# Relative bias of a banded attention: turned by a product with a flip matrix, or read from copies in DRAM with a shorter row step

## The chip, the core and the metric

One core of a Trainium2 chip runs the kernel. The metric is the device time in microseconds, the median of several runs. The engines are TensorE (PE; its weight loads are listed as PEld), VectorE (DVE), ScalarE (ACT), GpSimd (POOL), and SyncE (SP), which issues every DMA of this kernel. Each engine runs its own instructions in a fixed order and waits on semaphores for the others. 16 DMA engines move the data.

## The reference, cut to what matters

The kernel computes one layer of a hybrid encoder for a prompt of 2048 tokens and a sample of 64: an RMS norm, one input projection (1024 to 4096), banded attention with 8 heads of 64 in one half, a gated linear recurrence with 4 heads of 128 in the other, an output projection with a residual, and a last RMS norm. The change concerns the bias that is added to the attention scores. It depends on the clipped distance of query and key alone:

```python
def band_attention(q, k, v, rel, valid, rel_bias):
    idx = jnp.clip(rel, -REL_CLIP, REL_CLIP) + REL_CLIP
    bias = rel_bias[:, idx].astype(jnp.float32)
    s = jnp.einsum('bnqhd,bnkhd->bnhqk', q, k).astype(jnp.float32) * ATTN_SCALE + bias
    s = jnp.where(valid[None, :, None], s, NEG_INF)
    p = jax.nn.softmax(s, axis=-1).astype(v.dtype)
    return jnp.einsum('bnhqk,bnkhd->bnqhd', p, v)
...
rel = jnp.arange(CHUNK)[:, None] + WINDOW_ROWS - band[None, :]
```

REL_CLIP is 128. So for a block of 128 queries the bias is a band matrix: the same for every block, with each row shifted by one against the row above, and one constant for all keys that are 128 or more back.

## The kernel before

**Tiles and stages.** The 2048 + 64 tokens are cut into four stages of 512 (the second has the sample's 64 beside them, SUPER). In each stage the 32 column tiles of the input projection are taken one after the other (JOBS): four groups g, and in each the four projections of a recurrence head (hf, hq, hi, hg) and the four of a pair of attention heads (pg, pq, pk, pv). One projection of a 512-token block is 24 products of 128x128 by 512: weights and inputs are each split into a high and a low part in float32r, and three of the four combinations are summed. The first stage loads the weights from the input (wraw), splits them on DVE (high part, a cast) and POOL (low part, four subtractions), and stores both parts in DRAM (wd); the later stages load wd. The weight tiles w are a ring of four, the raw tiles a ring of two. Between the projections of a group PE does the attention of pairs and the recurrences of heads that are ready. In the last stage the output projection follows, stored as seven products a pair of row blocks.

**The order.** The program is written by hand in generators, and a planner (class Plan, lines 52 to 237) runs them at trace time. It keeps a clock, charges each instruction an estimated duration on its engine, and lets a generator go on when the time that it asked for has come: `yield t` waits for the planned time t, `yield "D", t` waits until t and until DVE's planned queue is less than 600 ns ahead. What comes out is a fixed order on each engine. A DMA is planned (lines 204 to 208) as 520 ns after its issue, its bytes at 370 per ns behind the transfers planned earlier, and 2000 ns to land. `tk` holds tokens for shared buffers: "ck" a work tile of 128 x 512, "g" one PSUM bank that the recurrences use for all their small products.

**The bias.** The host lays rel_bias out as one row of 383 numbers for each head: 127 times the value of the farthest distance, then 256 values in order of falling distance. `load_bias` (lines 816 to 847) makes the tile `bias` of a pair of heads, [128, 2, 640], with the negative of the bias. It is spawned by `open_` of each pair (line 909). In the first stage, four times in all, it builds the tile and stores it in DRAM (biasd); in the later stages it only loads it. The build:

- line 825: SP loads `win`, in which partition i and head h hold numbers i to i + 255 of the head's row. Each partition starts one further than the one above. The bias needs the opposite: partition i must start at 127 - i.
- line 827: SP loads `far`, the first number of each row, to all partitions.
- lines 830 and 831: DVE fills columns 0 to 383 with the constant, one operation for each head.
- lines 833 to 835: PE multiplies `win` by `flip` (ones on the other diagonal), which turns the order of the partitions round, into the bank "g".
- line 839: DVE copies the bank to columns 384 to 639 with its sign changed.
- lines 841 and 842: DVE sets the columns that a chunk may not see to a large number.
- line 846: SP stores the tile.

`softmax_rows` (line 1013) does not start before `bias_at`, the planned time of the finished tile; DVE adds the bias to the scores there. `flip` is made once by POOL (lines 474 to 476).

Of the kernel before, what the change touches and what calls it, by code (L numbers as in the profile page):

```python
# [8 lines left out]
F32 = mybir.dt.float32  # L9
# [3 lines left out]
ALU = mybir.AluOpType  # L13
# [4 lines left out]
P = 128  # L18
D = 1024
# [353 lines left out]
def hymba_step(  # L373
# [24 lines left out]
    C = Plan()  # L398
    act, dve, pool, pe, sp = (Queue(C, e, x) for e, x in (("A", nc.scalar), ("D", nc.vector), ("P", nc.gpsimd),
                                                          ("T", nc.tensor), ("S", nc.sync)))  # L400
# [4 lines left out]
    cst = ctx.enter_context(tc.tile_pool(name="cst", bufs=1))  # L405
    wk = ctx.enter_context(tc.tile_pool(name="wk", bufs=2))
    dr = ctx.enter_context(tc.tile_pool(name="dr", bufs=1, space=DRAM))
# [5 lines left out]
    def T(pool_, shape, dt, tag, **kw):  # L413
        uid[0] += 1
        C.name(homes.get(id(pool_), ""), tag, kw.get("bufs") or 1, f"{tag}_{uid[0]}")
        return pool_.tile(list(shape), dt, tag=tag, name=f"{tag}_{uid[0]}", **kw)

    def psum(tag, shape=(P, 512), bufs=1):
        return T(ps, shape, F32, tag, bufs=bufs)
# [22 lines left out]
    def mm32(out, w, x):  # L442
        pe.matmul(out, w, x, start=True, stop=True)

    tk = {k: Tok(C, n) for k, n in dict(acc=2, s_ps=1, tr=2, pv=1, g=1, pr=PRB, ph=2, sig=2, vT=2, mixa=2,
                                     w=WBUFS, raw=RAWB, xn=XNB, kv=1, q=1, sga=2, bias=1, gf=1, gi=1, gg=1,
                                     ck=1, slot=4, x4=0, x5=0, rec=1).items()}
# [1 line left out]

    ident = T(cst, [P, P], F32, "ident")  # L450
    make_identity(nc, ident)
    flip = T(cst, [P, P], F32, "flip")
    ones = T(cst, [P, P], F32R, "ones")
    mask = T(cst, [P, P], U32, "mask")
    eps_t = T(cst, [P, 1], F32, "eps")
# [12 lines left out]
    def constants():  # L468
        pool.memset(eps_t, EPS)
        pool.memset(one_t, 1.0)  # L470
        maskf = asb[0][:, 0]
        pool.memset(maskf, 1.0)
        dve.tensor_copy(ones, maskf)
        pool.memset(flip, 1.0)
        pool.affine_select(out=flip, in_=flip, pattern=[[1, P]], compare_op=ALU.is_equal, fill=0.0,
                           base=-(P - 1), channel_multiplier=1)
        pool.affine_select(out=maskf, in_=maskf, pattern=[[1, P]], compare_op=ALU.is_ge, fill=0.0,
                           base=0, channel_multiplier=-1)
        dve.tensor_copy(mask, maskf)
        pool.memset(reset, 1.0)  # L480
        pool.memset(reset.rearrange("p (b t) -> p b t", t=32)[:, :, 0:1], 0.0)
        pool.memset(asb[0], 0.0)
# [333 lines left out]
    def load_bias(sb, p, d):  # L816
        yield from tk["bias"].get()
        nb = d.bias = T(wk, [P, 2, 640], F32, "bias", bufs=1)
        if sb:
            sp.dma_start(nb, biasd[p])  # L820
            d.bias_at = C.dma(655)
            return
        yield from tk["ck"].get()
        win = T(wk, [P, 4, P], F32, "ck", bufs=1).rearrange("p (h a) c -> p h (a c)", h=2)
        sp.dma_start(win, bass.AP(rel_rev.tensor, 2 * p * 383, [[1, P], [383, 2], [1, 256]]))
        far = T(wk, [P, 2], F32, "far", bufs=1)
        sp.dma_start(far, bass.AP(rel_rev.tensor, 2 * p * 383, [[0, P], [383, 2]]))
        t = C.dma(400)
        yield "D", t
        for h in range(2):  # L830
            dve.tensor_scalar(nb[:, h, 0:384], reset[:, :384], 0.0, far[:, h : h + 1], ALU.mult, ALU.subtract)
        C.dve(600)
        yield from tk["g"].get()
        pw = psum("g")
        pe.matmul(pw, flip, win.rearrange("p h c -> p (h c)"), start=True, stop=True)
        tk["ck"].put()
        t = C.pe()
        yield "D", t
        dve.tensor_scalar(nb[:, :, 384:640], pw.rearrange("p (h c) -> p h c", h=2), -1.0, None, ALU.mult)
        tk["g"].put(1, C.dve())  # L840
        dve.memset(nb[64:128, :, 0:64], BIG)
        dve.memset(nb[0:64, :, 576:640], BIG)
        t = C.dve(900, t)
        d.bias_at = t
        yield t
        sp.dma_start(biasd[p], nb)
        C.dma(655)
# [38 lines left out]
    def pair_jobs(sb, p):  # L886
# [10 lines left out]
        def open_():  # L897

            yield from tk["kv"].get()
            d.kd = T(pa, [P, 2, WIN + NMAX], F32R, "kd")  # L900
            d.v = T(pa, [P, 9, 4, 64], F32R, "v")
            d.q = T(pa, [P, 2, QW], F32R, "q")
            if sb:
                cd = carry[sb - 1][p]
                sp.dma_start(f32(d.kd[:, :, 0:512]), cd[:, 0:2, :])
                sp.dma_start(f32(d.v[:, 0:4].rearrange("p t s d -> p (t s d)")),
                             cd[:, 2:4, :].rearrange("p a c -> p (a c)"))
                d.k_t = d.v_t = C.dma(1024)
            C.spawn(load_bias(sb, p, d), 1)
            if smp:  # L910
                pool.memset(f32(d.v[DEC:, 4 + WIN // P]), 0.0)
                C.spawn(sample_cache(d), 1)
# [1124 lines left out]
    def program():  # L2037


        dve.memset(g_in, 0.0)  # L2040
        constants()
        kroom = f32(T(pa, [P, 2, WIN + NMAX], F32R, "kd")).rearrange("p a c -> p (a c)")
        vroom = f32(T(pa, [P, 9, 4, 64], F32R, "v")).rearrange("p t s d -> p (t s d)")
# [252 lines left out]
```

## Time and profile before

| what | value |
|---|---|
| median of 3 runs | 1261.63 us |
| lowest, highest | 1260.84, 1261.96 us |
| the profiled execution: its time | 1260.86 us |
| its span, first to last instruction | 1259.0 us |
| granted TensorE clock | 0.999 |
| busy: PE, DVE, ACT, POOL | 98%, 71%, 56%, 30% |
| moved by DMA | 271.72 MB, 216 GB/s in the mean |

The rows of the profile name what an instruction writes and reads by the program's names (`g<-ck,flip` writes a tile g from ck and flip; `win` is a view of a tile ck and appears under that name). All instructions of engine queues are issued through one helper, so their line is that of the helper (L266), and one finds them by tile and not by line. A timeline row begins with the start and the duration in microseconds, has the engine, the operation, the tiles and the shape, then the count of like instructions merged in it, and in brackets how long the engine was idle before and what ended that. A float32 product appears as two records. Rows of DMA issues end with the count, the size of one and the median time from issue to landing; the rows of a queue have packets, megabytes and busy time as a share of 16 engines over the stretch asked for. Rows of one tile have the least, median and greatest duration in ns. Waits are given as total, times, longest.

### The profile page before, as it was taken

Reading aid. Unit: us, or ns where it says so; the run is one execution under the profiler, and the core shown is the slowest. Engines: PE = TensorE matmul, PEld = TensorE weight load, DVE = VectorE, ACT = ScalarE, POOL = GpSimd, SP = SyncE. Lnnn points to the kernel's source line nnn. Section 1 sums busy time; section 2 is a strip of 40 time slices with the busy share of each in tenths; the row PEclk is TensorE's granted clock in tenths of the full one; section 3 lists DMA queues with packets and bytes.
Section 4 is the critical chain, followed back from the end, with each engine's and each line's share of the span. In section 5 each row is a group of like instructions: output and inputs, shape, how many; then the busy total and the mean of one; then the engine's idle time right before and its main releaser. Section 6 shows DMA issues by size and latency. Waiting matters only on the chain. (4 is left out here: it accounts for less than half of the span.)

```text
span 1259.0 us, 22201 instructions
## 1 busy us (share of the span) xinstructions
PE 1238.8 (98%) x8120; PEld 1081.6 (86%) x8120; DVE 891.9 (71%) x1854; ACT 706.9 (56%) x1548; POOL 379.9 (30%) x703
## 2 busy tenths in 40 slices
PE   9999999999999999999999999999999999999997
PEld 8788887999999999998888888998888888788786
DVE  7786968766857678686584849783838574578886
ACT  6453546665656557575565656764636454753443
POOL 7766655111120210202533634110101104451110
PEclk9999999999999999999999999999999999999999
DMA  7887787645354554636879597646454657886331
GB/s 288 301 288 244 247 282 281 219 168 202 138 188 142 181 200 144 216 125 236 272 248 303 206 364 254 220 164 210 144 212 136 222 178 279 324 277 203 126 134 67
DMA packets 94830, 271.72 MB, mean 216 GB/s; under 512 B 10305, under 2 KB 43073, under 8 KB 77058
## 3 DMA queue, kind: packets, MB, share of 16 engines
q1 hardware_dynamic: 94722, 270.31, 61.4%
q8 instruction: 64, 1.05, 0.3%
q14 instruction: 44, 0.36, 0.1%
HBM read 186.66 MB, written 83.62 MB: 215 GB/s over the span
## 5 line engine op out<-in xcount | busy, mean ns | idle before, releaser
L266 PE MATMUL acc<-xh,w 128*128 128x512 f32 (+2 forms) x2720 | 568.4, 348 | 1.0 <-ACT sig L266 0.8
L266 PEld LDWEIGHTS acc<-xh,w 128*128 128x128 f32 x2720 | 436.7, 189 | 51.7 <-issue 1.4
L266 PE MATMUL acc<-xl,w 128*128 128x512 f32 (+2 forms) x1360 | 297.4, 348 | 0.0
L266 PEld LDWEIGHTS acc<-xl,w 128*128 128x128 f32 x1360 | 219.3, 189 | 24.9 <-issue 0.5
L266 POOL TENSOR_TENSOR mixa<-mixa,sga 128x256 f32<-128x256 f32 (+1 forms) x36 | 29.8, 828 | 334.8 <-DVE mixa L266 259.6
L266 DVE CUSTOM_DVE_ANT_0 pr<-s,bias 128x640 f32<-128x640 f32 (+5 forms) x144 | 100.7, 703 | 34.5 <-PE s L266 33.9
L266 ACT ACTIVATE pr<-pr,nm 128x640 f32<-128x640 f32 (+4 forms) x132 | 100.7, 763 | 39.0 <-DVE nm L266 37.9
L266 ACT CAST ph<-tr 128x512 fp32r<-128x512 f32 (+3 forms) x176 | 88.1, 507 | 59.7 <-PE tr L266 27.9
L266 POOL TENSOR_TENSOR w<-wraw,w 128x256 fp32r<-128x256 f32 x120 | 105.3, 906 | 46.9 <-DVE w L266 25.9
L266 DVE TENSOR_TENSOR ph<-tr,ph 128x512 fp32r<-128x512 f32 (+3 forms) x176 | 101.1, 589 | 10.0 <-ACT ph L266 8.8
L266 PE MATMUL pv<-ph,v 128*128 128x256 f32 (+2 forms) x344 | 97.2, 373 | 3.1 <-DVE ph L266 2.4
L266 PE MATMUL tr<-ident,pr 128*128 128x128 f32 x580 | 91.2, 273 | 2.4 <-DVE pr L266 1.2
L266 PEld LDWEIGHTS tr<-ident,pr 128*128 128x128 f32 x580 | 70.4, 140 | 16.6 <-issue 3.8
L266 ACT ACTIVATE sig<-acc 128x256 f32<-128x256 f32 (+2 forms) x86 | 42.7, 497 | 73.6 <-PE acc L266 73.3
L266 ACT COPY vT<-acc 128x512 f32<-128x512 f32 (+2 forms) x64 | 31.3, 488 | 71.2 <-PE acc L266 71.1
L266 DVE TENSOR_SCALAR pr<-pr,sm 128x640 f32<-128x640 f32 (+3 forms) x124 | 67.9, 547 | 4.4
L266 DVE TENSOR_TENSOR mixa<-mixa,pv 64x256 f32<-64x256 f32 (+1 forms) x144 | 56.8, 394 | 18.9 <-ACT mixa L266 14.7
L266 PEld LDWEIGHTS pv<-ph,v 128*128 128x128 f32 x344 | 57.4, 190 | 10.3 <-issue 2.0
L266 ACT ACTIVATE sig<-sig 128x512 f32<-128x512 f32 (+2 forms) x109 | 57.3, 528 | 10.0 <-DVE gk L266 7.3
L266 PE MATMUL s<-kd,q 128*128 128x320 f32 (+3 forms) x232 | 56.9, 315 | 0.2
L266 POOL TENSOR_TENSOR xn<-wraw,xn 128x256 fp32r<-128x256 f32 x48 | 37.8, 803 | 62.2 <-ACT xn L266 62.1
L266 PE MATMUL s<-kd,ql 128*128 128x320 f32 (+3 forms) x232 | 55.6, 309 | 0.0
(319 smaller groups left out, 2064.5 us busy)
## 6 DMA issues: line engine op xcount, KB each, us to landing
w<-wd SPq DMA_DIRECT2D x96, 1024.0 KB, 5.1
wd<-w SPq DMA_DIRECT2D x32, 1024.0 KB, 7.6
wraw<-in_w_in_dram SPq DMA_DIRECT2D x30, 512.0 KB, 5.5
wod<-xn SPq DMA_DIRECT2D x28, 512.0 KB, 5.0
xn<-in_x_prompt_dram SPq DMA_DIRECT2D x23, 512.0 KB, 5.5
bias<-biasd SPq DMA_DIRECT2D x12, 640.0 KB, 7.5
carry<-kd SPq DMA_DIRECT2D x12, 512.0 KB, 8.0
carry<-v SPq DMA_DIRECT2D x12, 512.0 KB, 5.2
```

The costliest lines, as they stand in the source:

```text
L266: r = f(*args, **kw)
```

## The change

`flip` and its two POOL operations go. In the first stage `load_bias` no longer loads `win` nor takes the tokens "ck" and "g". Instead a DMA copies each head's row of 383 numbers 128 times into a DRAM tile `same`, [2, 128, 383]; the source has a step of 0 over the copies. A second DMA reads `same` from element 127 on with a row step of 382, one less than a copy: partition i then starts at 127 + 382 i, which is 127 - i within copy i. It writes columns 384 to 639 of `bias` directly, and DVE changes the sign there in place. The far load is issued between the two DMAs, and the second is issued by the generator after the planned landing of the first. The operations of DVE on `far` are asked for at the planned time of that second issue, and the change of sign at its planned landing.

```diff
-    flip = T(cst, [P, P], F32, "flip")
...
-        pool.memset(flip, 1.0)
-        pool.affine_select(out=flip, in_=flip, pattern=[[1, P]], compare_op=ALU.is_equal, fill=0.0,
-                           base=-(P - 1), channel_multiplier=1)
...
-        yield from tk["ck"].get()
-        win = T(wk, [P, 4, P], F32, "ck", bufs=1).rearrange("p (h a) c -> p h (a c)", h=2)
-        sp.dma_start(win, bass.AP(rel_rev.tensor, 2 * p * 383, [[1, P], [383, 2], [1, 256]]))
+        same = T(dr, [2, P, 383], F32, f"rel{p}")
+        sp.dma_start(same, bass.AP(rel_rev.tensor, 2 * p * 383, [[383, 2], [0, P], [1, 383]]))
+        t = C.dma(400)
         far = T(wk, [P, 2], F32, "far", bufs=1)
         sp.dma_start(far, bass.AP(rel_rev.tensor, 2 * p * 383, [[0, P], [383, 2]]))
+        C.dma()
+        yield t
+        near = nb[:, :, 384:640]
+        sp.dma_start(near, bass.AP(same.tensor, same.offset + P - 1, [[382, P], [383 * P, 2], [1, 256]]))
         t = C.dma(400)
-        yield "D", t
+        yield "D", C.now
         for h in range(2):
             dve.tensor_scalar(nb[:, h, 0:384], reset[:, :384], 0.0, far[:, h : h + 1], ALU.mult, ALU.subtract)
-        C.dve(600)
-        yield from tk["g"].get()
-        pw = psum("g")
-        pe.matmul(pw, flip, win.rearrange("p h c -> p (h c)"), start=True, stop=True)
-        tk["ck"].put()
-        t = C.pe()
         yield "D", t
-        dve.tensor_scalar(nb[:, :, 384:640], pw.rearrange("p (h c) -> p h c", h=2), -1.0, None, ALU.mult)
-        tk["g"].put(1, C.dve())
+        dve.tensor_scalar(near, near, -1.0, None, ALU.mult)
         dve.memset(nb[64:128, :, 0:64], BIG)
         dve.memset(nb[0:64, :, 576:640], BIG)
         t = C.dve(900, t)
```

## The prediction

> **What bounds the kernel now.** I read the page's head first, then who TensorE (PE) waits for, then all that touches the removed matrix, then the order of time around the places where the bias is built.
>
> ```profile
> span 1259.0 us, 22201 instructions
> PE 1238.8 (98%) x8120; PEld 1081.6 (86%) x8120; DVE 891.9 (71%) x1854; ACT 706.9 (56%) x1548; POOL 379.9 (30%) x703
> q1 hardware_dynamic: 94722, 270.31, 61.4%
> mixd<-mixa SPq DMA_DIRECT2D x32, 128.0 KB, 2.2
> ck<-in_rel_bias_dram SPq DMA_DIRECT2D x4, 256.0 KB, 4.2
> ...
> DMA to landing us min/median/max: 3.2/4.6/8.1
> ...
> PE g L266 <- DVE bias L266: 0.9, 2, 0.4
> ```
>
> PE is busy for 98% of the span, so a microsecond taken out of its stream, or put into it as a stall, is about a microsecond of the end. Its waits are small; 0.9 us of them are for VectorE (DVE) copying the turned bias out of the g bank, which the next product in that bank needs. The DMA rows are used below (the one of landings is that of the far load). PE, DVE, ScalarE, GpSimd (POOL) and SyncE (SP) each run a fixed order that the planner wrote from its own estimates: an instruction that waits longer than planned holds all behind it on its engine.
>
> **What is removed.**
>
> ```profile
> L266 PE MATMUL g<-ck,flip x8: 591/592/607, 51.2 to 234.5; 128*128 128x512 f32 x8
> L266 POOL MEMSET flip<- x1: 204/204/204, 1.5 to 1.5; 128x128 f32 x1
> L266 POOL TENSOR_SCALAR_AFFINE_SELECT flip<-flip x1: 423/423/423, 1.8 to 1.8; 128x128 f32<-128x128 f32 x1
> ...
> 8.07 1.04 POOL L266 CAST w<-wraw 128x1024 fp32r<-128x1024 f32 x1 [4.48 <-DMA wraw<-in_w_in_dram]
> ...
> 107.53 0.41 PEld L266 LDWEIGHTS g<-ck,flip 128*128 128x128 f32 x2
> 108.17 0.19 PEld L266 LDWEIGHTS acc<-xh,w 128*128 128x128 f32 x1 [0.24 <-issue]
> 108.60 0.19 PEld L266 LDWEIGHTS acc<-xh,w 128*128 128x128 f32 x1 [0.24 <-issue]
> 108.83 1.34 PEld L266 LDWEIGHTS acc<-xl,w 128*128 128x128 f32 x6
> ```
>
> Four products with flip (eight records of 592 ns, which overlap). Their price is read from the weight loads: between the first flip load (107.53) and the second load of the projection behind it (108.60) lie 1.07 us, where one projection step takes 0.23 us ((1.34 - 0.19) / 5 in the row of six). So one product takes 1.07 - 0.23 = 0.84 us of PE, four take 3.4 us. With the 0.9 us of waits for the bank the gain is 4.3 us. POOL loses 0.20 + 0.42 us at 1.5 us, but its first work on a weight, at 8.07, waits 4.48 us for a DMA: zero. (Were POOL not waiting there, the two would be worth 0.6 us.) The final scaling on DVE reads SBUF in place of PSUM; I cost that at nothing, and at most at its whole present length it would be worth less than 0.7 us each time, off PE's path.
>
> **What is added.** Each of the four builds gets one DMA more: the window load (256 KB) gives way to a copy of DRAM to DRAM, which writes 2 x 128 x 383 x 4 = 392,192 bytes as 256 rows of 1532 bytes, and then a load of the window's size. The second reads what the first wrote, so SP must wait for the first to land before it issues the second. That is a new wait at the head of SP's queue, and the far load, issued between the two, shares the copy's DMA rings.
>
> The trace has no such copy, so I bound it. For the price of a packet, two stretches:
>
> ```profile
> q1 hardware_dynamic: 1681, 5.75, 84.1%
> ...
> q1 hardware_dynamic: 1324, 3.12, 55.9%
> ```
>
> From 96 to 116 us: 0.841 x 16 x 20 / 1681 = 160 ns a packet of 3421 bytes; from 229 to 246 us: 0.559 x 16 x 17 / 1324 = 115 ns of 2356. The line through both is 16 ns + 0.042 ns a byte; 1532 bytes then take 80 ns. Over the whole page it is 0.614 x 16 x 1259 / 94722 = 131 ns. The fixed part of a DMA is 1.8 us: the 128 KB store of mixd lands in 2.2 us, 0.4 of it data at some 370 bytes/ns.
>
> What matters most is how many engines carry it. The destination is [2, 128, 383]: its outermost count is 2, where every large transfer of the trace has 64 or 128 rows outermost. If shares are cut along the outermost count, two engines get 128 rows each: 128 x 80 ns = 10.2 us, landing 12.0 us after issue on idle rings; at 131 ns, 18.6 us. If all 16 take part, 16 x 80 ns = 1.3 us, landing in 3.1 us, no later than the window's 4.2. No row decides between these ends. I take two engines at 80 ns, because nothing in the code cuts the leading 2 any finer and the rows nearest in time give the 80, and keep 3.1 and 18.6 for the range.
>
> [...]
>
> **Where the lateness goes.** The planner charges the copy as if it ran at full rate (1.06 us of data and 2 us). That is what it charged for window and far load together (0.71 + 0.35 + 2), so the DVE operations on far will stand where they stand now:
>
> ```profile
> 35.75 0.33 SPq L266 DMA_DIRECT2D wraw<-in_w_in_dram  x1
> 36.13 0.47 SPq L266 DMA_DIRECT2D wd<-w  x1
> 36.70 0.42 SPq L266 DMA_DIRECT2D ck<-in_rel_bias_dram  x1
> 48.44 0.74 DVE L266 TENSOR_SCALAR bias<-reset,far 128x384 f32<-128x384 f32 x2
> 52.18 1.21 DVE L266 TENSOR_TENSOR q<-k,q 128x512 fp32r<-128x512 f32 x1 [1.80 <-POOL k L266]
> 54.37 0.63 PE L266 MATMUL g<-q,ones 128*128 128x512 f32 x2
> ...
> 96.31 0.43 SPq L266 DMA_DIRECT2D ck<-in_rel_bias_dram  x1
> 101.87 1.14 DVE L266 TENSOR_SCALAR bias<-reset,far 128x384 f32<-128x384 f32 x2 [1.00 <-DMA far<-in_rel_bias_dram]
> 102.93 0.28 DVE L266 COPY S<-g 128x128 f32<-128x128 f32 x1
> 104.98 0.69 DVE L266 CAST w<-wraw 128x1024 fp32r<-128x1024 f32 x1 [0.63 <-PE acc L266]
> 105.23 0.39 PE L266 MATMUL g<-bm,S 128*128 128x128 f32 x2
> ...
> 154.45 0.44 SPq L266 DMA_DIRECT2D ck<-in_rel_bias_dram  x1
> 159.17 1.75 DVE L266 TENSOR_SCALAR bias<-reset,far 128x384 f32<-128x384 f32 x2 [0.21 <-DMA far<-in_rel_bias_dram]
> 163.33 0.39 PE L266 MATMUL g<-bm,S 128*128 128x128 f32 x2
> ...
> 229.11 0.43 SPq L266 DMA_DIRECT2D ck<-in_rel_bias_dram  x1
> 234.55 0.75 DVE L266 TENSOR_SCALAR bias<-reset,far 128x384 f32<-128x384 f32 x2
> 237.21 0.87 DVE L266 TENSOR_TENSOR kd<-vT,kd 64x256 fp32r<-64x256 f32 x2
> 237.80 0.22 PE L266 MATMUL s<-kd,q 128*128 128x128 f32 x1
> ```
>
> At two of the four, DVE already waits for far (1.00 and 0.21 us): there is no cover in front. On two rings the far load stands behind the copy and lands some 0.4 us after it, at 12.4 us from the issue. Then:
> - Second pair: DVE comes to far 5.56 us after the issue (96.31 to 101.87), so it is 12.4 - 5.6 = 6.8 us late. Behind it in DVE's queue stand the state updates S, which PE's products with S wait for; these have about 2 us of room (S is there at 103.2, PE asks at 105.23). PE stalls 4.8 us.
> - Third pair: the same order, 154.45 to 159.17 is 4.7, late by 7.7; less 2, 5.7 us.
> - Fourth pair: 5.4, late by 7.0; the split of K behind it (237.21) feeds the score product at 237.80 with 0.2 us of room: 6.8 us.
> - First pair: 1.5 MB of a weight load and a weight store (35.75, 36.13) stand in the rings first, some 4.2 us of data, so the copy lands at about 52.8 and far at 53.2, against 48.44: 4.8 late. DVE then has 1.80 us idle (before 52.18), and 1.0 us lies between the end of that operation and the product at 54.37: PE stalls 2.0 us.
>
> Sum 19.3 us. The near load is issued when the copy has landed and comes 3.4 to 5 us later (issue 0.5, data 1.1, fixed 1.8, and up to 1.5 MB of weights queued between). DVE, itself late, reaches its scaling about then: I take 2 us at the fourth pair, where least work stands between far and near, and 0.7 at the others: 4 us. Both ends: 0 and 4 x 5 = 20.
>
> SP stands still for some 8 us each time (12.0 less the 3.7 after which the planner issues near). Behind it are weight loads, weight stores and mixd stores. The cast at 104.98 waits for PE to free a weight tile, not for its load: with four tiles the split is about three projections of 24 x 0.23 = 5.5 us ahead, 16 us of cover. I cost SP's wait at nothing; were that cover gone, it would be 8 us each time.
>
> **The sum.** 19.3 + 4.0 - 4.3 = +19.0 us. The profiled execution took 1260.86 us, 1259.0 of span and 1.9 around it: 1279.9. The median of the runs is 0.8 above the profiled one: 1281 us.
>
> **Rivals.**
> 1. The other side: the copy runs on all 16 engines and lands in 3.1 us. Far is not late, near lands about where it is planned, and the flip products are pure gain: 1261.6 - 4.3 = 1257.3, to 1261 if each near load still holds DVE by 1 us. It decides where far lands within 5 us of the issue. For it: the page's transfers all run near full rate. Against: the leading 2.
> 2. Two engines at the page's mean packet, 131 ns: the copy lands 6.6 us later each time, and with the room already used all of it reaches PE: 1281 + 26 = 1307. For it: each packet is read from DRAM and written to DRAM, on rows that start at odd multiples of 4 bytes, which no row of the trace prices. Against: the line through two stretches.
> 3. The stall is there but given back: PE, held, finds all later operands ready, and DVE's present idle time (1.80 us before 52.18 in the first pair) takes the lateness up in every pair except for what the gain pays: about 1262. Against: PE's waits now are so few that nothing is left to give back.
>
> **Chances.** Forecast 0.60, first rival 0.16, second 0.18, third 0.06. The forecast's own range is 1266 to 1296. The range for all runs from 1257 (the copy on 16 engines) to 1310 (131 ns a packet); what lies outside is a slower copy still, or gains above 4.3. A change under 0.2%, 2.5 us, cannot be told from none: faster 0.16, same 0.06, slower 0.78.
>
> **What would show it.** In the changed kernel's DMA table the copy should take some 12 us to land, the far load about as long where it took 4.6, and the DMA share should be low while they run. Among DVE's waits one for far should stand at 5 to 8 us, four times, and PE should show waits for DVE of 2 to 7 us at the four builds. SP should wait about 8 us for the copy each time. The flip rows should be gone, with PE's busy time lower by some 3 us apart from its stalls. A copy that lands in 3 to 4 us proves the forecast wrong and the first rival right; a late copy with no DVE wait behind it, the placing of far in DVE's order; PE waiting for weights, the cover.

## The result, and the profile after

| | before | after |
|---|---|---|
| median of 6 runs each | 1261.8 us | 1280.3 us |
| lowest, highest | 1260.84, 1263.05 us | 1275.55, 1282.65 us |
| the profiled execution: its time | 1260.86 us | 1280.82 us |
| its span | 1259.0 us | 1278.8 us |
| granted TensorE clock | 0.999 | 0.993 |

The ratio is 1.0139 with an interval of 1.0117 to 1.0161: slower by 18.5 us, where the prediction's sum was 19.0. The head of the changed kernel's page:

```profile
span 1278.8 us, 22186 instructions
PE 1243.4 (97%) x8112; PEld 1084.4 (85%) x8112; DVE 891.8 (70%) x1854; ACT 707.6 (55%) x1548; POOL 374.6 (29%) x705
...
...
q1 hardware_dynamic: 95754, 271.88, 60.2%
```

The flip rows are gone (8112 records of PE where there were 8120) and the queue has 1.57 MB more, four times 392 KB. PE's busy time has nevertheless grown, from 1238.8 to 1243.4 us, and the granted clock has fallen from 0.999 to 0.993. Of that more below.

**The copy.** SP's timeline shows when the copy (`rel`) was issued and when SP, which has to see it landed, came to the near load (`bias<-rel`); here the second and third pair, then the far load's own landing, and last a row of the windows view (one stretch of time: busy time of each engine, granted clock, share of the 16 DMA engines that was busy, GB/s) from the fourth pair, by when hardly anything but the copy and the small far load was under way:

```profile
100.11 0.67 SPq L266 DMA_DIRECT2D rel<-in_rel_bias_dram  x1
113.16 0.38 SPq L266 DMA_DIRECT2D bias<-rel  x1
...
163.33 0.64 SPq L266 DMA_DIRECT2D rel<-in_rel_bias_dram  x1
175.86 0.38 SPq L266 DMA_DIRECT2D bias<-rel  x1
...
DMA to landing us min/median/max: 12.0/12.0/12.0
...
252.00:254.00 2.00, 0.84 (x8) 0.63 (x6) 0.00 (x0) 0.41 (x2) 0.00 (x0) 1.00 0.13 45
```

113.16 - 100.11 = 13.05 and 175.86 - 163.33 = 12.53 us; the fourth pair took 13.8, the first, behind the weights, 16.1. The DMA share of 0.13 of 16 engines is 2.1 engines, so two are taken to carry the copy. Without the 1.8 us that were estimated as the fixed part, 12.53 us are then 128 packets of 84 ns on each, near the 80 that the line through two stretches gave. Far landed 12.0 us after its own issue where it took 4.6 before.

**Who waits.** The groups of waits, of DVE, SP and PE:

```profile
DVE bias L266 <- DMA far<-in_rel_bias_dram: 29.6, 4, 9.2
DVE w L266 <- DMA wraw<-in_w_in_dram: 2.5, 3, 1.8
DVE bias L266 <- DMA bias<-rel: 0.8, 2, 0.4
...
SPq L266 <- DMA rel<-in_rel_bias_dram: 25.8, 4, 7.2
...
PE acc L266 <- DVE sga L266: 5.8, 3, 2.8
PE g L266 <- DVE xl L266: 5.5, 5, 4.5
PE tr L266 <- DVE xn L266: 2.4, 2, 2.1
PE g L266 <- DVE q L266: 2.0, 1, 2.0
PE s L266 <- DVE kd L266: 1.2, 1, 1.2
PE g L266 <- DVE stp L266: 0.9, 3, 0.6
```

The six groups of PE make 17.8 us. The kernel before has one of them, xl, with 1.2 us; so 16.6 us are new, and the 0.9 us for the bank is gone. Place by place, from the timelines of DVE and PE around the last three builds:

```profile
113.29 0.75 DVE L266 TENSOR_SCALAR bias<-reset,far 128x384 f32<-128x384 f32 x2 [9.23 <-DMA far<-in_rel_bias_dram]
115.72 1.19 PE L266 MATMUL acc<-xh,w 128*128 128x512 f32 x4 [2.75 <-DVE sga L266]
...
176.01 0.75 DVE L266 TENSOR_SCALAR bias<-reset,far 128x384 f32<-128x384 f32 x2 [8.72 <-DMA far<-in_rel_bias_dram]
178.45 0.73 PE L266 MATMUL acc<-xh,w 128*128 128x512 f32 x2 [2.26 <-DVE sga L266]
...
255.38 0.75 DVE L266 TENSOR_SCALAR bias<-reset,far 128x384 f32<-128x384 f32 x2 [7.31 <-DMA far<-in_rel_bias_dram]
257.33 1.09 PE L266 MATMUL g<-ident,xn 128*128 128x128 f32 x4 [4.49 <-DVE xl L266]
269.85 1.07 PE L266 MATMUL tr<-ident,xn 64*128 64x64 f32 x8 [2.12 <-DVE xn L266]
```

Each time DVE stands 7 to 9 us for far, and 2.0 to 2.4 us after it goes on, PE goes on too, having been out of work for 2.3 to 4.5 us. (At the first pair it is 4.4 us for far and 0.8 for PE.) The waits for `kd` (1.2 us, at 66.91) and `q` (2.0 us, at 125.24) belong to the first and the second build too: each comes 9 to 12 us after PE's first stall there. At the second and third pair the first that PE lacks is not a product with S but the next projection: its bank acc is free only when DVE has used the last one for `sga`.

**The clock.** In steps of 2 us around three of the last four stalls, and then in three stretches of 3.41 us (the column before the last two is the granted clock):

```profile
178.00:180.00 2.00, 0.93 (x3) 0.50 (x4) 1.64 (x5) 0.12 (x1) 2.00 (x4) 0.92 0.91 275
180.00:182.00 2.00, 2.00 (x10) 2.00 (x11) 1.67 (x4) 0.00 (x0) 0.66 (x1) 0.50 1.03 436
182.00:184.00 2.00, 2.00 (x11) 1.82 (x11) 1.91 (x4) 0.73 (x2) 0.10 (x1) 0.73 1.01 420
...
254.00:256.00 2.00, 0.00 (x0) 0.00 (x0) 0.62 (x2) 0.00 (x0) 0.00 (x0) 0.69 0.11 36
...
260.00:262.00 2.00, 2.00 (x13) 2.00 (x13) 0.92 (x2) 1.92 (x6) 0.00 (x0) 0.60 0.85 274
...
270.00:272.00 2.00, 1.86 (x17) 1.66 (x17) 1.93 (x9) 1.73 (x5) 0.00 (x0) 0.96 0.58 232
274.00:276.00 2.00, 2.00 (x13) 2.00 (x12) 0.70 (x3) 1.18 (x3) 0.00 (x0) 0.69 0.00 0
...
111.41:114.83 3.42, 1.56 (x7) 0.94 (x6) 1.21 (x3) 1.77 (x3) 0.00 (x0) 1.00 0.41 138
176.27:179.68 3.41, 0.73 (x2) 0.30 (x2) 2.96 (x8) 1.79 (x3) 1.80 (x3) 1.00 0.79 223
268.43:271.84 3.41, 1.85 (x16) 1.65 (x17) 3.34 (x9) 3.29 (x11) 0.00 (x0) 1.00 0.71 284
```

The clock falls to one half (0.50 from 180 to 182 us) and comes back. A window of 0.92 held 2 x 0.08 / 0.5 = 0.32 us of it, so the first fall began at 179.68 and ended at 182 + 2 x 0.27 / 0.5 = 183.08; the second ran from 254.76 to 261.60, the third from 271.84 to 275.24. They lasted 3.40, 6.84 and 3.40 us, and their beginnings lie 75.08 and 17.08 us apart, which is 22 and 5 times 3.41 (75.08 / 22 = 3.413). So in this trace the falls begin and end on a grid of 3.41 us. The second pair's stall of 2.75 us had no fall behind it: a step of the grid ends at 114.83 (19 steps before 179.68) and splits it, with 1.86 us ahead and 0.89 behind. How much idle time in a step brings a fall these rows do not tell: PE worked 1.56 us in the step up to 114.83, which had no fall behind it, and 1.85 us in the step up to 271.84, which had one. Before the first fall PE worked 0.73 us of the step, so a step ahead of a fall need not be idle throughout. While PE worked it lost at most 5.5 us: half of 3.40, of 261.60 - 257.33 and of 3.40.

The account then: 16.6 + 5.5 - 3.4 (flip products) - 0.9 (bank) = 17.8 of the 19.8 us between the spans. The other 2.0 us are no further waits: span less busy time of PE grew by 15.2 us (from 20.2 to 35.4), no more than these waits. They stand in PE's busy time, and what they are is not shown.

### The profile page after: what moved, and what is told of

Its sections match the earlier page's. It is cut to its first block, busy times and chain, and to the rows that moved or that the text cites. A ratio compares the mean times of both kernels' runs of the same rounds, so it can differ in the third digit from the quotient of the medians.

```text
span 1278.8 us, 22186 instructions
## 1 busy us (share of the span) xinstructions
PE 1243.4 (97%) x8112; PEld 1084.4 (85%) x8112; DVE 891.8 (70%) x1854; ACT 707.6 (55%) x1548; POOL 374.6 (29%) x705
## 5 line engine op out<-in xcount | busy, mean ns | idle before, releaser
L266 POOL TENSOR_TENSOR w<-wraw,w 128x256 fp32r<-128x256 f32 x120 | 102.5, 881 | 63.8 <-DVE w L266 54.8
L266 DVE TENSOR_SCALAR pr<-pr,sm 128x640 f32<-128x640 f32 (+3 forms) x124 | 70.5, 569 | 4.4
L266 POOL TENSOR_TENSOR k<-ob 128x512 f32<-128x512 f32 (+2 forms) x20 | 18.5, 927 | 131.6 <-ACT ob L266 128.3
```

The source lines that it names most:

```text
L266: r = f(*args, **kw)
```

## The experiments

Ten kernels. Ratios are to runs of the kernel before on the same chip; the diffs are against the changed kernel.

**Rows outermost.** The copy's tile is laid out with the 128 rows outermost and both heads in each row.

```diff
-        same = T(dr, [2, P, 383], F32, f"rel{p}")
-        sp.dma_start(same, bass.AP(rel_rev.tensor, 2 * p * 383, [[383, 2], [0, P], [1, 383]]))
+        same = T(dr, [P, 2, 383], F32, f"rel{p}")
+        sp.dma_start(same, bass.AP(rel_rev.tensor, 2 * p * 383, [[0, P], [383, 2], [1, 383]]))
...
-        sp.dma_start(near, bass.AP(same.tensor, same.offset + P - 1, [[382, P], [383 * P, 2], [1, 256]]))
+        sp.dma_start(near, bass.AP(same.tensor, same.offset + P - 1, [[2 * 383 - 1, P], [383, 2], [1, 256]]))
```

> The copy is laid out copy by copy, [128, 2, 383]: same bytes, same 256 rows of 1532 bytes, but 128 is its outermost count. Theory A (the copy was slow because its outermost count of 2 gave it two DMA engines): it lands in 3 to 5 us, far in under 6 us, DVE's waits for far fall from 29.6 us to under 4, PE's waits for DVE at the builds vanish, the granted clock goes back to 0.999, and the time is 1257 to 1262 us. Theory B (it is the dependent pair itself, a DRAM write that a load must wait for): SP still waits 5 us or more for the copy each time and the time stays above 1270. Theory C (the order that the planner draws anew costs the time, not any wait): 1275 to 1283, since the planner draws nearly the same order.

Measured 1256.55 us (1255.56 to 1257.76), ratio 0.995 [0.9937, 0.9963], clock 0.998. The DMA table of this run:

```profile
rel<-in_rel_bias_dram SPq DMA_DIRECT2D x4, 383.0 KB, 6.1
```

The same bytes land in 6.1 us in place of some 13, a little later than theory A's 3 to 5. Theories B and C fall with the time; SP's waits for the copy are at most 3.6 us. DVE still waits 5.2 us for far, in two of the builds, but PE no longer waits behind it. The whole loss is gone and 6.0 us of gain remain between the medians (4.5 between the profiled spans, 1254.5 against 1259.0, where 4.3 were worked out): this version beats both kernels. What the change set out to do, to trade the flip product for a copy, does pay; only the outermost 2 did not. It also gives a second measure of the loss: with the same 8112 records PE is busy for 1235.7 us here and 1243.4 in the change. So of the 24.3 us between these two spans 16.6 are idle time of PE, and 7.7 are longer busy time for the same work, of which the falls of the clock explain at most 5.5.

**The same rows, walked the other way.** The run above moved the rows too. Here they lie as in the change, and only the order of the copy is turned.

```diff
-        sp.dma_start(same, bass.AP(rel_rev.tensor, 2 * p * 383, [[383, 2], [0, P], [1, 383]]))
+        sp.dma_start(same.rearrange("h r c -> r h c"), bass.AP(rel_rev.tensor, 2 * p * 383, [[0, P], [383, 2], [1, 383]]))
```

> The copy's rows lie in DRAM exactly as in the change (head by head, 128 rows each, the near load with its row step of 382 words untouched); only the order in which the copy walks them is turned, 128 outermost in place of 2. Theory A (the outermost count of 2 puts the copy on two of the 16 engines, and that alone is the loss): 1254 to 1259 us, as the run with rows outermost, the copy landing within 6 to 7 us of its issue, PE's waits for DVE at the four builds gone. Rival L (the layout of the rows, one head's 196 KB after the other's, is what makes the copy or the near load slow): 1275 to 1283 us as the change.

Measured 1258.35 us (1257.46 to 1264.24), ratio 0.9985 [0.9972, 0.9998], clock 0.998.

```profile
rel<-in_rel_bias_dram SPq DMA_DIRECT2D x4, 383.0 KB, 7.0
```

Theory A holds, and the layout is not the cause of the loss: one outermost count makes the difference between 13 and 7.0 us, and between 1280 and 1258. The planner reckons with the same copy in both, so its order is not the cause either. But against the kernel before, this run gains 1.9 us by its ratio where rows outermost gained 6.3, and its runs fall into two groups, 1257.5 to 1258.7 and 1261.5 to 1264.2; the one profile doesn't tell why.

**The loss in one pair alone.** Flip (which is made again) for the first three pairs, the change for the fourth; the diff leaves out what is only indented.

```diff
+        if p == 3:
             same = T(dr, [2, P, 383], F32, f"rel{p}")
...
+        else:
+            yield from tk["ck"].get()
+            win = T(wk, [P, 4, P], F32, "ck", bufs=1).rearrange("p (h a) c -> p h (a c)", h=2)
```

> Only the fourth pair is built by copies (outermost count 2); the three others keep the flip product. Theory A: the fourth pair alone loses what the changed kernel's trace shows from its fourth build on, where the shift against the kernel before grows from 12.3 to 20.0 us: 1267 to 1273 us. Theory C (the order drawn anew): no relation to that figure.

Measured 1268.67 us (1268.0 to 1269.68), ratio 1.0052 [1.0039, 1.0064], clock 0.996: 6.5 us of loss, inside theory A's range. PE's timeline and the windows:

```profile
245.75 1.11 PE L266 MATMUL g<-ident,xn 128*128 128x128 f32 x4 [5.94 <-DVE xl L266]
...
242.00:244.00 2.00, 0.00 (x0) 0.00 (x0) 1.41 (x4) 0.00 (x0) 0.00 (x0) 0.85 0.31 82
...
250.00:252.00 2.00, 2.00 (x18) 2.00 (x17) 0.51 (x4) 1.63 (x4) 0.00 (x0) 0.94 0.82 318
```

One stall of 5.94 us, and one fall of the clock, from 243.4 to 250.2: 6.8 us, again two steps of 3.41. PE worked in 4.5 us of it and lost half, 2.2. 5.9 + 2.2 - 0.8 for the one product saved is 7.3, and the span is longer by 1266.2 - 1259.0 = 7.2. One pair's account closes within 0.1 us.

**VectorE asked late.** SP and the copy are left as they are; the operations with far are asked for 9.5 us after the planned landing of near, so that they stand further back in DVE's order.

```diff
-        yield "D", C.now
+        t = C.dma(400) + 9500.0
+        yield "D", t
```

> As the changed kernel, with the copy of outermost count 2 and the SP wait before the second load, but both groups of DVE operations are asked for 9.5 us later in the planner's clock, so that DVE's order has them where the data lands. Theory A, with the loss through DVE's fixed order: DVE waits for far fall under 4 us in all, PE has no waits at the builds, clock 0.999, 1257 to 1263 us, although SP still waits some 26 us for the copies. Theory D (it is SP's wait, with the weight loads and stores behind it): 1274 to 1283, as the changed kernel.

Measured 1270.86 us (1268.08 to 1272.44), ratio 1.006 [1.0046, 1.0075], clock 0.994: between the two theories. More than half of the loss is gone. The waits, and two rows of the first build from the timelines of SP and DVE:

```profile
DVE w L266 <- DMA wraw<-in_w_in_dram: 13.9, 4, 5.5
...
PE s L266 <- DVE nm L266: 4.5, 2, 2.6
PE s L266 <- DVE kd L266: 3.6, 1, 3.6
...
43.27 1.50 SPq L266 DMA_DIRECT2D wraw<-in_w_in_dram  x1
...
54.11 0.69 DVE L266 CAST w<-wraw 128x1024 fp32r<-128x1024 f32 x1 [5.09 <-DMA wraw<-in_w_in_dram]
```

DVE waits for far no more, and with that the larger part of the loss has gone. But now DVE waits 13.9 us for weights: a load issued at 43.27, behind the copy, is there only when the cast at 54.11 can begin, 10.8 us later, where the median landing of the changed kernel's weight loads is 5.6. In the kernel before DVE has no such wait among its own. The late bias operations then stand right ahead of the first scores, and PE waits there. So SP's wait and the late landings behind the copy do make DVE wait, which the change hid by DVE's standing still anyway; how much of the 7.6 us that are left is theirs, and how much comes from the new place of the bias operations, this run doesn't separate.

**Far first.** The far load is issued ahead of the copy, otherwise as the change.

```diff
+        far = T(wk, [P, 2], F32, "far", bufs=1)
+        sp.dma_start(far, bass.AP(rel_rev.tensor, 2 * p * 383, [[0, P], [383, 2]]))
         same = T(dr, [2, P, 383], F32, f"rel{p}")
...
```

> The far load is issued ahead of the copy. Theory A: far lands in 3 to 5 us and DVE no longer waits for it, but DVE then waits 5 to 9 us at the change of sign for the second load, which still lands 16 to 18 us after the copy's issue: the loss moves, and the time is 1268 to 1282 us. Theory E (only far, caught in the rings behind the copy, matters): 1257 to 1263.

Measured 1273.93 us (1273.32 to 1278.67), ratio 1.0094 [1.0079, 1.011], clock 0.994. DVE's waits:

```profile
DVE bias L266 <- DMA bias<-rel: 7.2, 3, 5.6
```

None for far is left; 7.2 us for near has come, 5.6 at one place. A third of the loss goes, and the time lies in theory A's range: the wait moves to the next operation that needs the copy, and one wait of 4.1 us for a weight load comes with it. Far was the first victim, not the cause.

**All asked late.** Near's issue too is put 9.5 us later, and DVE follows.

```diff
-        yield t
+        yield t + 9500.0
```

> As the changed kernel, with the copy of outermost count 2, but the generator waits 9.5 us longer before it issues the second load, and with it asks DVE for its work: the planner now reckons with a copy of 13 us, so neither SP nor DVE meets the wait. In the kernel in which only DVE was asked later the time was 1270.9 us, with SP still waiting 23.8 us for copies. Theory A with D (the late landing costs through both fixed orders, DVE's directly and SP's by late weight loads that DVE's casts wait for): SP's wait for the copies and DVE's for far both under 4 us in all, clock 0.998 or more, 1256 to 1262 us. Theory F (the copy on two rings delays the loads behind it, whatever is planned): 1266 to 1274.

Measured 1282.46 us (1279.67 to 1283.76), ratio 1.0157 [1.0143, 1.0171], clock 0.991: no theory had this. No wait for far or near is left on DVE and one of 4.3 us for a copy on SP; DVE waits 9.1 us for weights. What came instead, at the third pair, from the timelines of SP, ACT and PE:

```profile
185.31 5.73 SPq L266 DMA_DIRECT2D far<-in_rel_bias_dram  x1
191.15 2.73 SPq L266 DMA_DIRECT2D xn<-in_x_prompt_dram  x3
...
201.89 1.06 ACT L266 ACTIVATE ck<-xn 128x1024 bf16<-128x1024 f32 x1 [9.20 <-DMA xn<-in_x_prompt_dram]
...
208.41 3.52 PE L266 MATMUL acc<-xh,w 128*128 128x512 f32 x8 [6.90 <-DVE gq L266]
260.02 1.22 PE L266 MATMUL acc<-xh,w 128*128 128x256 f32 x4 [6.28 <-ACT vT L266]
```

The planner, with other times, has put the loads of x right behind the copy. SP needs 5.73 us only to issue far, the x loads start at 191.15 and land 10 us later, ACT has stood 9.20 us for them, and PE runs dry for 6.90. It is the same copy ahead of what is issued next, with another victim. The second stall, 6.28 us up to 260.02, begins before the fourth copy is issued (255.61) and has no wait for a DMA ahead of it in the rows of DVE or ACT from 252 us on; what of the new order makes it was not settled. So waiting longer did not help here, in part because the copy still lay ahead of whatever was issued next, and in part for a reason that stays open.

**One copy for all, early.** The rows of all eight heads are copied in one DMA at the start, 128 outermost; the builds only load.

```diff
+        sp.dma_start(same, bass.AP(rel_rev.tensor, 0, [[0, P], [1, 8 * 383]]))
...
+    same = T(dr, [P, 8, 383], F32, "rel")
...
-        sp.dma_start(same, bass.AP(rel_rev.tensor, 2 * p * 383, [[383, 2], [0, P], [1, 383]]))
-        t = C.dma(400)
...
-        yield t
...
```

> All eight rows of all pairs are copied by one DMA of 128 rows of 12,256 bytes near the start, and the four builds only load from it; SP waits for nothing. All theories but C: the pure gain of the four products and bank waits, 4.3 us: 1256 to 1259 us, unless the 1.6 MB copied at 17 us delay the first weights (then up to 1262). Theory C: anything between 1255 and 1283.

Measured 1264.55 us (1262.21 to 1266.37), ratio 1.0012 [1.0004, 1.0021], clock 0.996: slower than was expected. The edit kept `yield "D", C.now`, so DVE was asked for far at the moment of its issue:

```profile
DVE bias L266 <- DMA far<-in_rel_bias_dram: 17.6, 3, 7.9
PE acc L266 <- DVE gg L266: 6.6, 2, 4.3
```

No copy stands ahead of far here, and DVE waits for it 17.6 us all the same, and PE 6.6 behind that. The place in DVE's order counts too, whatever the copy takes.

**The same, asked at near's landing.** `yield "D", t` in place of `yield "D", C.now` in the kernel above.

> One early copy of all rows, as before in the study, but DVE's work on far is asked for at the planned landing of the load, not at once: there the wait of DVE for far (17.6 us in all) was of my own making. Theory A: DVE's wait for far falls under 3 us and the time to 1255 to 1258 us. If it stays at 1262 to 1266, the early copy itself costs the time.

Measured 1256.05 us (1255.17 to 1257.89), ratio 0.9952 [0.994, 0.9965], clock 0.998. DVE's waits for far and PE's stalls are gone, and by the ratios the one changed line is worth 0.6%, 7.6 us. The time is that of the rows outermost, so two ways lead to a gain of some 6 us between the medians. Between the profiled spans it is 3.8 us here and 4.5 there, near the 4.3 that were worked out for the flip products and their bank; where the rest of the 6 comes from is not shown.

**Rows outermost, asked at near's landing.** The first experiment with the same later asking.

> The run with 128 outermost, and VectorE's two calls with far asked at the near load's planned landing in place of at once. Theory A (with the copy on 16 engines what VectorE still waits for far, 5.2 us in two waits, holds nothing that TensorE needs): 1254.5 to 1258 us, the same within 0.15% as without the later asking. Rival W (those two waits still cost what they last): 1250 to 1253 us.

Measured 1259.99 us (1258.34 to 1261.85), ratio 0.9987 [0.9976, 0.9998], clock 0.999. Neither theory: it is slower than with the operations asked at once, by 4.7 us in the ratios and 3.1 between the profiled spans. DVE's waits for far are gone and paid nothing; instead PE waits for DVE 1.4 us for `pr` and 1.3 for `nm`, where the first experiment had 0.2 and none. No wait of PE's stood behind the 5.2 us that DVE waited for far in the first experiment, and shifting its work later cost something.

**Filling the stalls.** Idle products (the identity on a constant, into the bank g) are put into PE's order behind each build, 0, 3, 3 and 5 of them, meant to keep PE at work where it stalls.

```diff
+    def fill(n):
+        yield from tk["g"].get()
+        pw = psum("g")
+        for _ in range(n):
+            pe.matmul(pw, ident, reset, start=True, stop=True)
+        tk["g"].put(1, C.pe())
...
+        C.spawn(fill((0, 3, 3, 5)[p]), 0.5)
```

> The changed kernel with useless products of 0.85 us each in PE's order at the second, third and fourth build (3, 3 and 5 of them, 9.35 us in all), where PE stalls anyway. Theory G (part of the loss is the granted clock, at a half for some 4 us after a stall): the products take the place of the stalls, the clock stays at 0.997 or more, and the time falls to 1273 to 1278 us. Theory H (the clock is worth nothing): 1280 to 1283; if the products do not fall into the stalls, 1286 to 1290.

Measured 1278.57 us (1276.09 to 1279.9), ratio 1.0123 [1.0108, 1.0139], clock 0.996 against the change's 0.993: between the two theories, and so undecided by its median. One row of DVE at the third pair, and PE's at the third and fourth:

```profile
172.23 0.82 DVE L266 TENSOR_SCALAR bias<-reset,far 128x384 f32<-128x384 f32 x2 [1.27 <-DMA far<-in_rel_bias_dram]
...
182.26 2.79 PE L266 MATMUL g<-reset,ident 128*128 128x512 f32 x6
...
243.70 4.56 PE L266 MATMUL g<-reset,ident 128*128 128x512 f32 x10
256.18 1.08 PE L266 MATMUL g<-ident,xn 128*128 128x128 f32 x4 [1.52 <-DVE xl L266]
```

At the second pair the fill came behind the stall and did nothing for it; a stall of 2.64 us up to 115.71 had a fall behind it here, from 116.3, where 2.75 us had none in the change. At the third pair the stall and the fall are gone, but not because of the fill: the order has moved, DVE comes to far so late that it waits 1.27 us where it waited 8.72, and the fill stands behind that. At the fourth the fill lies in front of the stalls, which shrink from 4.49 and 2.12 us to 1.52 and 0.97, and a fall came after these two. That a stall brings the fall is borne out by the third pair and by the runs without stalls (0.998 in both that gained). The runs of this one kernel bear out that the clock is worth something: the two with a granted clock of 0.996 took 1279.6 and 1279.9 us, the two with 0.999 and 1.0 took 1276.1 and 1277.6. What the falls cost by themselves was not measured, since a run without them may also have had shorter stalls.

## Right or wrong, by the prediction's steps

- **Two engines.** Right, and shown: a DMA share of 2.1 engines while the copy runs nearly alone, 12.5 to 13.8 us to land without the weights ahead, where 12.0 was worked out, and about half of that with the walk turned. A packet comes to 84 ns against 80.
- **Far stands behind the copy.** Right: at the last three pairs DVE goes on with far 12.7 to 14.0 us after the copy's issue, where 12.4 was put, with its waits 4.4, 9.2, 8.7 and 7.3 where 4.8, 7.8, 7.9 and 7.0 follow from the prediction's lateness with the waits that were there already.
- **PE's stalls.** The mechanism was right, the size too large: 16.6 us in all where 19.3 and 4.0 were put. Pair by pair PE stood 2.0, 4.9, 2.9 and 6.6 us where 2.0, 4.8, 5.7 and 6.8 were put. At the third pair the step "less 2, 5.7 us" was mis-sized. The prediction looked at the products with S; the instruction that stopped first was the projection whose bank waits for `sga`, and what ran before that was more than 2 us of room. The good agreement at the first two pairs is partly luck: 1.2 and 2.0 us of it came 9 to 12 us after the first stall, at `kd` and `q`, which the prediction did not name for these pairs.
- **Near.** 4.0 us were put for it. DVE waited 0.8 us for near in all, since it was late itself; but the far-first run shows what is behind that: 7.2 us, as soon as far is out of the way.
- **SP's wait at nothing.** Half wrong. SP waited 25.8 us in four, less than the 8 us each that were put, and in the change itself DVE's casts lost only 2.5 us to late weights. But the cover of 16 us was counted from SP's order alone; the weights also land late behind the copy, and the run with DVE asked late shows 13.9 us of waits for them. The longest, 5.46 us up to 182.91, is for a load that SP issued only at 178.16, when its own wait for the copy was over: there SP's order itself had no cover left.
- **What was left out.** The clock: no step had it, and it costs up to 5.5 us. So the good agreement of the sum, +19.0 forecast and +18.5 measured, is partly luck: the stalls were put 6.7 us too high, and the clock and 2.0 us of PE's busy time that no row explains stand in for them.
- **The rivals.** Two engines at 131 ns a packet falls with the 84. That the stall is given back falls with the waits. The first rival's condition was made true in two ways: of its price, 1257.3 to 1261, the turned walk with 1258.35 us lies inside and rows outermost with 1256.55 a little below. Its 3.1 us for the landing did not come: the copy took 6.1 and 7.0 us there, among the weights' traffic.

## To carry to other kernels

Ahead of a copy, look at its outermost count: a leading 2 on both sides made a 392 KB copy take 13 us where 128 took 6 to 7, with the same bytes and rows. Cost a slow transfer not only by who reads it but by what is issued behind it (here a load of 1 KB landed in 12.0 us where it took 4.6), and don't expect full relief from moving one of its readers: of three such moves one gave back somewhat more than half of the loss, one a third and one nothing, and each made other instructions wait. Count a stall of TensorE with what the clock takes afterwards; here one stall of 5.9 us cost 8.

## What had not been expected of the hardware

**Issuing waits too.** The far load, 1 KB, took SP hardly any time to issue before, and long in the change. Its rows by tile (count, then least, median and greatest ns of the issue), before and after:

```profile
L266 SPq DMA_DIRECT2D far<-in_rel_bias_dram x4: 496/530/1876, 37.2 to 229.6; - x4
```

```profile
L266 SPq DMA_DIRECT2D far<-in_rel_bias_dram x4: 2488/3945/5761, 37.1 to 242.1; - x4
```

A median of 3945 ns against 530 (670 in the run with rows outermost, and 444 where far goes ahead of the copy), and the weight loads behind it took 1.4 to 2.2 us to issue where 0.33 is usual. While the copy runs SP is held already at the issue of the next DMA, before any wait for a semaphore; what holds it there, no row names.

**The clock's grid.** Falls of 3.4 or 6.8 us on a grid of 3.41 us go with two stalls of like length costing differently by where they lie: at the second pair 2.75 us, split by the grid, brought no fall in the change, and 2.64 us brought one in the run with the fill, where the step before the fall, from 112.89 to 116.31, holds the whole stall. It may also be part of why the changed kernel's runs spread over 7 us where those before spread over 2: its two runs with a granted clock of 0.995 took 1275.6 and 1275.9 us, the four with 0.993 or 0.994 took 1279.8 to 1282.7. That is more than the clock alone can give, since 0.002 of 1279 us is 2.6 us, so the stalls must have differed too.
